# Tokens ahead of the modulation matrix: reordering the opening of an encoder trunk

## The chip, the cores and the metric

The kernel is one program on one core of a Trainium2 chip. The metric is the device time of one execution in microseconds (us). Three runs of the kernel before gave 2377.03, 2378.3 and 2380.01 us; the median, 2378.3 us, is the time before.

In the profile PE is the matmul engine and PEld its weight load, DVE the vector engine, ACT the scalar engine, POOL the GpSimd engine and SP the engine that issues nearly all DMAs.

## The reference

The trunk has two layers (sequence 1024, width 1024, batch 1, all float32). What matters here is the start of the first one:

```
cond = silu(c)                                   # c: 1024 numbers
mod = cond @ w_mod[l] + b_mod[l]                 # w_mod[l]: 1024 x 6144
sh_a, sc_a, gt_a, sh_f, sc_f, gt_f = split(mod)  # six rows of 1024
h = rms_norm(x, g_attn[l]) * (1 + sc_a) + sh_a   # x: 1024 tokens x 1024
proj = h @ w_in[l]                               # w_in[l]: 1024 x 2048
...                                              # three attention groups, w_o, residual
h = rms_norm(x, g_ffn[l]) * (1 + sc_f) + sh_f    # then a SwiGLU FFN, residual
```

Before any projection can begin, a feature needs its shift `sh_a` and scale `sc_a`, that is two columns of `w_mod` multiplied by `cond`, and a token needs its root mean square.

## The kernel before

Everything is held with features on the 128 partitions: `xt[:, n, t]` is token `t` of feature chunk `n` (eight chunks of 128). A float32 product is made of three products of parts: each operand is split into a high part that the PE multiplies and a low part that is the rest, and `mm3` adds high x high, low x high and high x low. `hh` and `hl` are the high and low part of the normalised, modulated `h`; `whi` and `wlo` those of a weight.

The stretch that the change touches is the opening, which is written out by hand: `pin` (L744 to L899) makes PE, ACT, DVE and SP each run their instructions in the order in which the code issues them. POOL has its own order. A wait of one instruction therefore holds everything behind it on the same engine.

In the opening the kernel does the following.

- `load_vecs` issues on POOL's queue four small loads for each layer (bias and gains, 72 rows of 128), and `turn_vecs` transposes them on PE so that a chunk's bias and gain stand on partitions. `turn_vecs(0)` and `turn_vecs(1)` stand together.
- `gm_load(i)` loads a 1 MB tile of `w_mod`: half of the 1024 rows, shift and scale columns of two feature chunks. Eight such tiles, in three buffers, make the 1024 features. `gemv_half(i, kd)` multiplies it by `cond`: for the first `kd` of its four row blocks DVE multiplies and adds into `ga`, and for the rest PE does it with matmuls of one column (`ps_m`). `columns` then adds `ga` with one more set of one-column matmuls, and `gemv_finish` adds the bias and makes the scale `gsc` on DVE. In the trace each of these one-column matmuls of the program stands as two rows.
- `x_load` loads 128 tokens (512 KB). `x_square` sums their squares on ACT, `x_turn_first` transposes them on PE (`ps_x`) and copies them to `xt`, `x_rms` and `spread` make the reciprocal root mean square of the first 512 tokens and spread it over the partitions (`ps_r`, copied to `rb`).
- `h_blocks` makes two chunks of `h`: on DVE `nt` = token x scale x reciprocal root, on ACT `hh` = `nt` + shift, on DVE `hl` = `nt` + shift - `hh`.
- `wc_stage` loads two chunks' rows (512 KB) of the 512 columns of `w_in` for attention group C, `w_high` splits them. `c_first(n)` multiplies chunk `n` of the first 512 tokens with them: three passes of four 128x512 matmuls into the four banks `ps_c`. `a_stage`, `a_high` and `a_first` do the same for two column blocks of group A (`ps_ab`).
- `keep_busy(n)` issues `n` 128x512 matmuls whose result nobody reads (`ps_idle`).

The chunks come in pairs: `gemv_finish(0)`, `h_blocks(0, ..., (0, 1))`, `c_first(0)`, `c_first(1)` and so on. `c_first(4)` is the first product of the fifth chunk; from there on the code of before and after is the same. Later in the opening `gains_load` loads the head gains `g8` (tile `g`) and `c_norm_first` multiplies by them on DVE; `skA` is a 1 MB copy between DRAM buffers that needs a small table `skr`, which POOL stores once a `gm` buffer has come free for it.

Of the kernel before, what the change touches and what calls it, by code (L numbers as in the profile page):

```python
# [10 lines left out]
F32 = mybir.dt.float32  # L11
# [74 lines left out]
def trunk(ctx: ExitStack, tc, A, C, out):  # L86
# [544 lines left out]
    def gemv_half(i, kd=3):  # L631
# [18 lines left out]
        if s:  # L650
            return lambda: columns(gas.pop(p), ones, False, True)

    def gemv_finish(p):
# [33 lines left out]
    def wc_stage(kp):  # L687
        st = stage()
        for dst, v in w_in_src(0, C_COLS, kp)(parts(st, 2)):
            sp.dma_start(dst, v)  # L690
        wcs.append(st)

    def c_first(n, passes=range(3)):

# [58 lines left out]
    wc_stage(0)  # L753
    gm_load(2)
# [20 lines left out]
    keep_busy(10)  # L775
    gemv_half(0)
    gm_load(3)
    wc_stage(1)
    keep_busy(8)
    x_square(0, 0, xns[0][0], rxs[0])  # L780
    x_square(0, 1, xns[0][1], rxs[0])
    columns = gemv_half(1)
    gm_load(4)
    keep_busy(4)
    columns()
    turn_vecs(0, v0)
    turn_vecs(1, v1)
    gemv_finish(0)
    for copy in x_turn_first(xns[0], 0, range(4)):
        copy(dve.tensor_copy)  # L790
    x_square(0, 2, xns[0][2], rxs[0])
    keep_busy(3)
    x_square(0, 3, xns[0][3], rxs[0])
    copies = x_turn_first(xns[0], 1, range(4))
    copies[0](dve.tensor_copy)
    x_rms(rxs[0])
    rows = spread(rxs[0], 0, psl)
    low = w_high()
    copies[1](act.copy)
    keep_busy(6)  # L800
    h_blocks(0, rows, (0, 1), low)
    a_stage(0)
    for copy in copies[2:]:
        copy(act.copy)
# [3 lines left out]
    c_first(0)  # L808
    gemv_half(2, 2)
    gm_load(5)  # L810
    c_first(1, (0, 1))
    low = w_high()
    columns = gemv_half(3, 2)
    gm_load(6)
    columns()
    c_first(1, (2,))
    low()
    wc_stage(2)
    gemv_finish(1)
    a_low = a_high(0)  # L820
    for j in (0, 1):
        xns[1].append(x_load(1, j))
    h_blocks(0, rb, (2, 3))
    c_first(2)
    a_low()
    pssA = [psl.tile([P, 512], F32, name="ps_ab", tag="mm") for _ in range(2)]
    gemv_half(4)
    gm_load(7)
    wc_stage(3)
    for j in (2, 3):  # L830
        xns[1].append(x_load(1, j))
    c_first(3)
    low = w_high()
    columns = gemv_half(5)
    low()
    a_stage(1)
    columns()
    gemv_finish(2)
    a_first(0, 0)
    a_first(0, 1)  # L840
    h_blocks(0, rb, (4, 5))
    c_first(4)
    x_square(1, 0, xns[1][0], rxs[1])
    x_square(1, 1, xns[1][1], rxs[1])
# [1740 lines left out]
```

## Time and profile before

| what | value |
|---|---|
| time, median of three runs | 2378.3 us (2377.03 to 2380.01) |
| the profiled execution's own time | 2376.24 us |
| its span, first to last instruction | 2374.4 us |
| mean granted PE clock | 0.997 |
| PE busy, share of the span | 98% |
| DVE, ACT, POOL busy | 74%, 50%, 33% |
| DMA packets, bytes | 307416, 358.01 MB |

The span is what the profile covers; 1.84 us of the execution's time lie around it. Nearly all operations are issued through one helper, so their source line is L49 and they are told apart by the names of their tiles. A timeline row gives the start, the length of the (merged) group, the engine, the operation, what it writes and reads, its shape, how many instructions it holds, and in brackets how long the engine was idle before it and what ended that.

### The profile page before, as it was taken

To read this page: it belongs to the slowest core of one execution; us is meant where nothing else is said; L and a number is where in the kernel's file an instruction comes from. 1 tells how busy PE (TensorE), PEld (TensorE's weight loads), DVE (VectorE), ACT (ScalarE), POOL (GpSimd) and SP (SyncE) were. 2 spreads that over 40 slices of the span, in tenths; PEclk is the share of its full clock that TensorE was granted. 3 is DMA by queue.
4 is the path that set the end of the run, shared out by engine and by line. 5 is a ranking of instruction groups with operands and counts; after the bars stand their busy time and mean duration, and the time that the engine had idled before them with its cause. 6 is when DMAs were issued, how large, how long until landed. Compare 5 with 4: busy or idle time off the path is not lost. (4 is left out here: it accounts for less than half of the span.)

```text
span 2374.4 us, 33475 instructions
## 1 busy us (share of the span) xinstructions
PE 2327.5 (98%) x11804; PEld 1961.2 (83%) x11804; DVE 1754.3 (74%) x2753; ACT 1184.7 (50%) x2261; POOL 787.0 (33%) x747
## 2 busy tenths in 40 slices
PE   9999999999999999999999999999999999999998
PEld 7888888888788888788888889988888888888886
DVE  6877998868857687595767689987796674537865
ACT  4422888844543333344533158896454333334443
POOL 1530446710344444200145124574025443430001
PEclk9999999999999999999999999999999999999999
DMA  8666407163345444685434861332634443339633
GB/s 279 181 204 207 148 9 206 46 208 104 117 149 164 155 138 151 209 247 178 152 104 132 245 187 28 84 111 80 221 101 130 153 154 107 98 102 292 217 120 111
DMA packets 307416, 358.01 MB, mean 151 GB/s; under 512 B 51996, under 2 KB 223868, under 8 KB 307248
## 3 DMA queue, kind: packets, MB, share of 16 engines
q1 hardware_dynamic: 290752, 346.26, 46.7%
q10 hardware_dynamic: 16128, 9.44, 1.5%
q8 instruction: 93, 1.52, 0.3%
q14 instruction: 75, 0.61, 0.1%
q0 software_dynamic: 368, 0.17, 0.0%
HBM read 270.84 MB, written 88.63 MB: 151 GB/s over the span
## 5 line engine op out<-in xcount | busy, mean ns | idle before, releaser
L49 PE MATMUL ps_d<-wpt 128*128 128x512 f32 x1848 | 423.7, 390 | 1.0 <-ACT wpt L49 0.7
L49 PEld LDWEIGHTS ps_d<-wpt 128*128 128x128 f32 x1848 | 345.7, 188 | 74.4 <-issue 3.0
L49 POOL TENSOR_SCALAR pr<-pr,rs 128x1024 f32<-128x1024 f32 (+2 forms) x248 | 190.4, 783 | 188.3 <-DVE rs L49 170.8
L49 POOL TENSOR_TENSOR sg<-sg,u 128x512 f32<-128x512 f32 x82 | 128.4, 1567 | 349.3 <-ACT sg L49 221.6
L49 PE MATMUL pv<-pt,vs 128*128 128x256 f32 x1088 | 176.0, 296 | 16.5 <-DVE y L49 13.8
L49 DVE TENSOR_TENSOR pt<-T,pt 128x512 fp32r<-128x512 f32 x272 | 177.5, 680 | 7.0 <-ACT pt L49 5.8
L49 ACT CAST wpt<-w 128x512 fp32r<-128x512 f32 x154 | 95.7, 621 | 172.4 <-PE ps_d L49 155.0
L49 ACT CAST pt<-T 128x512 fp32r<-128x512 f32 x272 | 151.6, 586 | 42.5 <-PE T L49 41.0
L49 ACT COPY u<-ps_w 128x512 f32<-128x512 f32 x128 | 75.1, 587 | 193.0 <-PE ps_w L49 190.2
L49 DVE SCALAR_TENSOR_TENSOR acc<-wmt,condT,acc 128x512 f32<-128x512 f32 (+1 forms) x98 | 113.9, 1170 | 75.3 <-DMA wmt<-in_w_mod_dram 74.8
L49 DVE TENSOR_TENSOR wpt<-w,wpt 128x512 fp32r<-128x512 f32 x154 | 108.9, 707 | 81.5 <-ACT wpt L49 81.5
L49 POOL TENSOR_TENSOR wpt<-ws,wpt 128x512 fp32r<-128x512 f32 x80 | 111.1, 1390 | 171.1 <-ACT wpt L49 126.0
L49 PEld LDWEIGHTS pv<-pt,vs 128*128 128x128 f32 x1088 | 142.1, 189 | 29.9 <-DVE y L49 25.5
L49 PE MATMUL T<-identr,pr 128*128 128x128 f32 x1176 | 160.8, 273 | 0.8 <-DVE pt L49 0.4
L49 PEld LDWEIGHTS T<-identr,pr 128*128 128x128 f32 x1176 | 137.8, 140 | 15.5 <-ACT edge L49 1.0
L49 ACT CAST wpt<-ws 128x512 fp32r<-128x512 f32 x176 | 107.7, 622 | 52.7 <-issue 22.9
L49 DVE TENSOR_TENSOR wpt<-graw,wpt 128x512 fp32r<-128x512 f32 x154 | 110.2, 715 | 17.3 <-ACT wpt L49 17.3
L49 ACT CAST wpt<-graw 128x512 fp32r<-128x512 f32 x154 | 95.0, 617 | 54.6 <-DMA graw<-gpd 48.9
L49 DVE TENSOR_TENSOR wpt<-ws,wpt 128x512 fp32r<-128x512 f32 x96 | 84.5, 889 | 47.8 <-ACT wpt L49 47.6
L49 DVE TENSOR_TENSOR ws<-wr 128x512 f32<-128x512 f32 x88 | 81.0, 920 | 50.2 <-POOL wpt L49 46.4
L49 DVE TENSOR_REDUCE rs<-sC 128x1 f32<-128x1024 f32 x88 | 107.2, 1220 | 12.6 <-PE sC L49 11.6
L49 PE MATMUL ps_w<-ht3h,wpt 128*128 128x512 f32 x352 | 108.9, 391 | 2.5 <-ACT sg L49 2.5
(306 smaller groups left out, 5936.5 us busy)
## 6 DMA issues: line engine op xcount, KB each, us to landing
wr<-in_w_gu_dram SPq DMA_DIRECT2D x92, 512.0 KB, 4.3
gpd<-sg SPq DMA_DIRECT2D x154, 256.0 KB, 4.4
graw<-gpd SPq DMA_DIRECT2D x76, 512.0 KB, 3.6
w<-in_w_down_dram SPq DMA_DIRECT2D x110, 256.0 KB, 5.3
wmt<-in_w_mod_dram SPq DMA_DIRECT2D x48, 512.0 KB, 5.6
qk<-qkd SPq DMA_DIRECT2D x44, 512.0 KB, 7.0
wst<-in_w_o_dram SPq DMA_DIRECT2D x32, 512.0 KB, 4.2
wmt<-in_w_mod_dram SPq DMA_DIRECT2D x64, 256.0 KB, 4.1
```

The lines of the kernel that those rows point to most:

```text
L49: ins = op(*args, **kwargs)
```

## The change

The change rewrites the opening up to `c_first(4)`.

- The first 512 tokens are loaded ahead of `w_mod`. The first four feature chunks get their own `w_mod` tiles (`gm_one(n)`: all 1024 rows, shift and scale columns of one chunk, 1 MB in four loads of 256 KB, rows of 512 bytes), and their rows of `w_in` come one chunk at a time (`wc_half`). The other four chunks keep the tiles of before.
- The class `One` does a chunk's gemv: `add` on DVE, `col` and `total` on PE. In chunk 0 six of the eight row blocks go to PE, in chunks 1 to 3 three.
- `turn` multiplies tokens by the reciprocal root ahead of the scale. `finish` then makes `hh` in one ACT instruction (scale and shift together); POOL makes the same value in full (`ht`) and `low` subtracts.
- The fillers become 8, 2, 1, 1, 2, 3, 3 and 2 in place of 10, 8, 4, 3 and 6. One `a_first` moves between other work, and `gemv_half(4)` puts two row blocks on PE in place of one.

```diff
+    def gm_one(n):
+        gm = gms["one", n] = stp.tile([P, KC, 2, P], F32, name="gm", tag="gm", bufs=3)
+        for k in (0, 4):
+            for g in range(2):
+                c0 = g * 1024 + n * P
+                rows = A["w_mod"][0, k * P : (k + 4) * P, c0 : c0 + P]
+                sp.dma_start(
+                    gm[:, k : k + 4, g, :], rows.rearrange("(k p) n -> p k n", p=P)
+                )
+    class One:
...
+        def turn(self, rows):
+            self.xr = stp2.tile([P, H], F32, name="nt", tag="nt", bufs=3)
+            dve.tensor_tensor(out=self.xr, in0=xt[:, self.n, 0:H], in1=rows, op=ALU.mult)
+        def finish(self):
...
+            dve.tensor_tensor(
+                out=m[:, :, n : n + 1], in0=self.ps[:, :, None], in1=v[:, :, n : n + 1],
+                op=ALU.add,
+            )
+            dve.scalar_tensor_tensor(
+                out=sc, in0=mods[0][:, 8 + n : 9 + n], scalar=1.0,
+                in1=vecs[0][:, 48 + n : 49 + n], op0=ALU.add, op1=ALU.mult,
+            )
+            act.activation(hh[:, n, 0:H], self.xr, AF.Identity, bias=sh, scale=sc)
+            self.t = stp2.tile([P, H], F32, name="ht", tag="ht", bufs=1)
+            pool.tensor_scalar(
+                out=self.t, in0=self.xr, scalar1=sc, scalar2=sh, op0=ALU.mult, op1=ALU.add
+            )
+        def low(self):
+            sub(hl[:, self.n, 0:H], self.t, f32(hh[:, self.n, 0:H]))
...
-    gm_load(0)
-    gm_load(1)
     xns = [[x_load(0, j) for j in range(4)], []]
+    gm_one(0)
+    wc_half(0)
+    gm_one(1)
+    wc_half(1)
+    gm_one(2)
+    wc_half(2)
     v0, v1 = load_vecs(0), load_vecs(1)
...
+    for n in range(1, 4):
+        two.add(0, 1, 2)
+        low = w_high_half(n)
+        c_first(n - 1, (0,))
+        two.col(3)
+        c_first(n - 1, (2,))
+        two.add(4, 5)
+        two.col(6)
+        c_first(n - 1, (1,))
+        two.col(7)
+        two.total()
+        two.finish()
+        if n < 3:
+            keep_busy(3)
+            one, two = two, One(n + 1)
+            two.turn(rb)
+            low()
+            one.low()
+            if n == 1:
+                a_stage(0)
+            gm_load(3 + n)
+        else:
+            low()
+            two.low()
...
+    keep_busy(2)
     c_first(4)
```

Where the instructions stand now. PE's program before, from the transposed vectors to the first products of group C (`pst` a transposed vector tile, `ps_x` transposed tokens, `ps_r` the spread root, `ps_c` group C, `ps_m` a gemv):

```order
L49 MATMUL pst<-identr,v_138 128x72
L49 MATMUL pst<-identr,v_143 128x72
L49 MATMUL ps_x<-identr,xn 128x128 x16
L49 MATMUL ps_idle<-identr 128x512 x3
L49 MATMUL ps_x<-identr,xn 128x128 x16
L49 MATMUL ps_r<-identr,rx 128x128 x4
L49 MATMUL ps_idle<-identr 128x512 x6
L49 MATMUL ps_c<-whi,hh 128x512 x4
```

PE's program after, the same place:

```order
L49 MATMUL ps_x<-identr,xn 128x128 x16
L49 MATMUL pst<-identr,v_152 128x72
L49 MATMUL pst<-identr,v_157 128x72
L49 MATMUL ps_idle<-identr 128x512 x2
L49 MATMUL ps_x<-identr,xn 128x128 x8
L49 MATMUL ps_m<-condT,gm 128x1 x4
L49 MATMUL ps_x<-identr,xn 128x128 x4
L49 MATMUL ps_r<-identr,rx 128x128 x4
L49 MATMUL ps_m<-condT,gm 128x1 x4
L49 MATMUL ps_x<-identr,xn 128x128 x4
L49 MATMUL ps_idle<-identr 128x512
L49 MATMUL ps_m<-condT,gm 128x1 x4
```

The first half of the token transposes moved ahead of the vectors, the second half and the spread stand behind them, and the first chunk's gemv is spread between them.

PE's program after, from the end of the first chunk's gemv through one turn of the loop over chunks:

```order
L49 MATMUL ps_m<-onesr,ga 128x1 x2
L49 MATMUL ps_idle<-identr 128x512 x2
L49 MATMUL ps_c<-whi,hh 128x512 x4
L49 MATMUL ps_m<-condT,gm 128x1 x2
L49 MATMUL ps_c<-wlo,hh 128x512 x4
L49 MATMUL ps_m<-condT,gm 128x1 x2
L49 MATMUL ps_c<-whi,hl 128x512 x4
L49 MATMUL ps_m<-condT,gm 128x1 x2
L49 MATMUL ps_m<-onesr,ga 128x1 x2
L49 MATMUL ps_idle<-identr 128x512 x3
```

Each turn holds one chunk's three passes and the next chunk's gemv, and ends with three fillers ahead of the next chunk's first product; before, two chunks' passes followed one another.

The difference on PE at the fifth chunk (`ps_ab` is group A, the last `ps_c` rows are `c_first(4)`):

```order
 L49 MATMUL ps_ab<-hh,hl 128x512
 L49 MATMUL ps_ab<-hl,hh 128x512
+L49 MATMUL ps_m<-onesr,ga 128x1 x4
+L49 MATMUL ps_idle<-identr 128x512 x2
 L49 MATMUL ps_c<-whi,hh 128x512 x4
 L49 MATMUL ps_c<-whi,hl 128x512 x4
```

The last matmuls of the third pair's gemv, which stood ahead of both `a_first`, now stand behind them, right ahead of `c_first(4)`, with two fillers between.

SP's queue before, from the last weight loads of the opening but one to the copy `skA`:

```order
L49 DMA wst<-in_w_in_dram 128x8x128 x2
L49 DMA g_518<-in_gq_ax_dram 128x6x64
L49 DMA g_518<-in_gk_ax_dram 128x2x64
L49 DMA cst<-const_rope_dram 128x128 x4
L49 DMA t_530<-in_t_table_dram 32x6
L49 DMA skA_91<-skr 512x1x512
```

SP's queue after, the same place:

```order
L49 DMA wst<-in_w_in_dram 128x8x128
L49 DMA skA_91<-skr 512x1x512
L49 DMA wst<-in_w_in_dram 128x8x128
L49 DMA g_555<-in_gq_ax_dram 128x6x64
L49 DMA g_555<-in_gk_ax_dram 128x2x64
L49 DMA cst<-const_rope_dram 128x128 x4
```

The copy `skA`, which waits for POOL's table, moved from behind the head gains to ahead of them.

More of the change, by code (lines that the diff above doesn't have):

```diff
@@ L774, in trunk @@
     dve.tensor_copy(condT, pst[:, :KC])
[L775 to L778, printed above, removed]
     keep_busy(8)
[L780 to L785, printed above, removed]
+    for j in range(4):
+        x_square(0, j, xns[0][j], rxs[0])
+    for copy in x_turn_first(xns[0], 0, range(4)):
+        copy(dve.tensor_copy)
     turn_vecs(0, v0)
     turn_vecs(1, v1)
[L788 to L790 removed]
@@ L791, in trunk @@
[L791 to L794, printed above, removed]
+    keep_busy(2)
+    one = One(0)
+    copies = x_turn_first(xns[0], 1, (0, 1))
     copies[0](dve.tensor_copy)
     x_rms(rxs[0])
+    copies[1](act.copy)
+    one.col(0, 1)
+    x_turn_first(xns[0], 1, (2,))[0](act.copy)
     rows = spread(rxs[0], 0, psl)
[L798 to L801, printed above, removed]
@@ L802, in trunk @@
-    a_stage(0)
-    for copy in copies[2:]:
-        copy(act.copy)
+    one.turn(rows)
+    one.col(2, 3)
+    x_turn_first(xns[0], 1, (3,))[0](act.copy)
     rb = stp2.tile([P, H], F32, name="rb", tag="rb", bufs=2)
     act.copy(rb, rows)
-    pssC = [psl.tile([P, 512], F32, name="ps_c", tag="mm") for _ in range(T0)]
[L808 to L811, printed above, removed]
-    low = w_high()
[L813 to L821, printed above, removed]
-        xns[1].append(x_load(1, j))
[L823 to L833, printed above, removed]
+    one.add(4, 5)
+    keep_busy(1)
+    one.col(6, 7)
+    keep_busy(1)
+    one.total()
@@ L834, in trunk @@
+    wcs = wcs[2:]
+    wc_stage(2)
+    a_high(0)()
+    gm_load(6)
+    wc_stage(3)
+    pssA = [psl.tile([P, 512], F32, name="ps_ab", tag="mm") for _ in range(2)]
+    gemv_half(4, 2)
+    c_first(3, (0, 1))
+    low = w_high()
+    gm_load(7)
+    for j in range(4):
+        xns[1].append(x_load(1, j))
+    c_first(3, (2,))
+    a_first(0, 0)
     columns = gemv_half(5)
```

63 lines of the change are left out of this document (59 added, 4 removed).

## The prediction

> **What bounds the kernel.** I read the page's busy shares first, then the busy times by stretch, then PE's timeline of the opening with what ended its waits, then the other engines at those places.
>
> ```profile
> span 2374.4 us, 33475 instructions
> PE 2327.5 (98%) x11804; PEld 1961.2 (83%) x11804; DVE 1754.3 (74%) x2753; ACT 1184.7 (50%) x2261; POOL 787.0 (33%) x747
> ```
>
> The profiled execution took 2376.24 us, 2.1 us under the median 2378.3. PE is full. The next view gives the busy time of each engine in a stretch (PE first); the last three fields are the granted clock, the DMA share and GB/s.
>
> ```profile
> 5.00:10.00 5.00, 5.00 (x23) 4.13 (x22) 1.99 (x3) 0.00 (x0) 1.54 (x4) 1.00 1.07 355
> 27.00:28.00 1.00, 1.00 (x6) 0.83 (x5) 1.00 (x2) 0.00 (x0) 0.00 (x0) 1.00 1.14 291
> 45.00:50.00 5.00, 5.00 (x28) 4.27 (x27) 4.82 (x7) 4.35 (x8) 1.75 (x2) 1.00 0.79 274
> 70.00:75.00 5.00, 5.00 (x24) 4.10 (x23) 3.72 (x7) 1.84 (x5) 0.72 (x1) 1.00 0.61 209
> ```
>
> From the fifth chunk on (44.97 us, below) PE has no gap up to 75 us, and the code behind that point is the same in both kernels. So I take it that what the change is worth is read at one place: when `c_first(4)` starts. PE's timeline up to there:
>
> ```profile
> 12.81 1.05 PE L49 MATMUL ps_m<-onesr,ga 128*128 128x1 f32 x8 [0.63 <-DVE ga L49]
> 13.72 0.32 PE L49 MATMUL pst<-identr,v 72*128 72x72 f32 x2
> 13.88 3.23 PE L49 MATMUL ps_x<-identr,xn 128*128 128x128 f32 x16
> 16.76 1.37 PE L49 MATMUL ps_idle<-identr 128*128 128x512 f32 x3
> 17.97 1.91 PE L49 MATMUL ps_x<-identr,xn 128*128 128x128 f32 x16
> 19.72 0.60 PE L49 MATMUL ps_r<-identr,rx 128*128 128x128 f32 x4
> ...
> 21.92 1.18 PE L49 MATMUL ps_c<-whi,hh 128*128 128x512 f32 x4 [0.20 <-ACT hh L49]
> 22.93 1.07 PE L49 MATMUL ps_c<-whi,hl 128*128 128x512 f32 x4
> 23.84 1.19 PE L49 MATMUL ps_c<-wlo,hh 128*128 128x512 f32 x4
> 24.87 1.84 PE L49 MATMUL ps_m<-condT,gm 128*128 128x1 f32 x16
> 26.57 1.16 PE L49 MATMUL ps_c<-whi,hh 128*128 128x512 f32 x4
> ...
> 30.19 1.03 PE L49 MATMUL ps_m<-onesr,ga 128*128 128x1 f32 x8
> 31.08 1.83 PE L49 MATMUL ps_c<-wlo,hh 128*128 128x512 f32 x4
> 33.21 1.89 PE L49 MATMUL ps_c<-whi,hh 128*128 128x512 f32 x4 [0.30 <-ACT hh L49]
> 34.94 1.09 PE L49 MATMUL ps_c<-whi,hl 128*128 128x512 f32 x4
> ...
> 42.12 0.48 PE L49 MATMUL ps_ab<-hh 128*128 128x512 f32 x1
> ...
> 44.97 1.07 PE L49 MATMUL ps_c<-whi,hh 128*128 128x512 f32 x4
> ```
>
> PE has 31 fillers (10 + 8 + 4 + 3 + 6 in the code) ahead of 21.92 and from there to 44.97 (23.05 us) only useful work with 0.30 us of waiting. Prices by the distance from one start to the next: four 128x512 products 0.91 (22.93 to 23.84), so 0.23 each; a one-column matmul of the program (two trace rows) 0.21 (24.87 to 26.57 for eight); a token transpose 0.11 (17.97 to 19.72 for 16), 0.18 in the slower stretch at 13.88; the spread 0.35; a filler there 0.46 (1.37 for three).
>
> The slower stretches are seen in the granted clock. The next view counts the one-column matmuls alone (first value after the length: their PE time; third from the end: the clock):
>
> ```profile
> 10.87:14.28 3.41, 1.33 (x11) 1.16 (x10) 0.00 (x0) 1.00 1.03 376
> 14.28:17.70 3.42, 0.00 (x0) 0.00 (x0) 0.15 (x1) 0.50 1.05 370
> 24.52:27.94 3.42, 1.84 (x16) 1.94 (x16) 0.00 (x0) 1.00 1.11 327
> 27.94:31.35 3.41, 2.73 (x24) 2.83 (x24) 0.10 (x1) 1.00 1.05 321
> 31.35:34.76 3.41, 0.00 (x0) 0.00 (x0) 0.07 (x1) 0.50 1.02 325
> ```
>
> The clock halves for 3.41 us after a stretch in which one-column matmuls and waits together held 1.33 + 0.63 = 1.96 us, or 2.73 us. It does not after 1.84 us.
>
> **The change, part by part.** I follow the new PE order to `c_first(4)`.
>
> *Loads.* From the first use of 1 MB of matrix and of the first tokens I get when data can be there:
>
> ```profile
> 6.61 0.49 DVE L49 TENSOR_SCALAR ga<-gm,condT 128x512 f32<-128x512 f32 x1 [3.12 <-DMA gm<-in_w_mod_dram]
> 24.88 2.33 DVE L49 SCALAR_TENSOR_TENSOR ga<-gm,condT,ga 128x512 f32<-128x512 f32 x3
> ```
>
> 1.05 MB at 355 GB/s are 2.95 us, so data run 3.65 us behind the clock. Tokens (2.1 MB) are there at 9.6; the first chunk's tile at 12.5 to 13.1 (355, or 291 GB/s, the lowest rate shown, for it), and each further 1.31 MB takes 3.7 to 4.4 us: chunk 3 by 23.6 to 26. All of that is ahead of its use below, so the loads themselves cost nothing; the earlier tokens and tiles are the change's gain only if nothing else is late.
>
> *What is late instead: the small vectors.* In the new order eight token transposes, the spread and the whole first gemv stand behind both `turn_vecs`, layer 1's too. POOL issues those loads one by one:
>
> ```profile
> 5.52 0.50 POOL L49 DMA_DIRECT2D v<-in_g_group_dram  x1
> DMA to landing us min/median/max: 3.8/5.9/6.6
> ```
>
> (the second line is the tile view of `v`). The last one lands at 5.52 + 5.9 to 6.6, 11.4 to 12.1; I take 11.8. Before, PE came to them at 13.72 and waited for nothing. Now PE is through the first 16 transposes near 9 and stands. From 11.8: vectors 0.2, two fillers and eight transposes at half clock (the wait halves it) 0.9 + 1.4, gives 14.3; four one-column matmuls 0.85, four transposes 0.44, spread 0.35, then 0.85, 0.44, filler 0.23, 0.85, filler 0.23, total of two 0.43, gives 19.0.
>
> *The way from a gemv's end to the first product.* Its stations are seen once before:
>
> ```profile
> 31.25 0.16 DVE L49 TENSOR_TENSOR mod<-ps_m,vecs 128x4 f32<-128x4 f32 x1 [2.91 <-PE ps_m L49]
> 31.45 0.16 DVE L49 SCALAR_TENSOR_TENSOR gsc<-mod,vecs 128x2 f32<-128x2 f32 x1
> 31.65 1.42 DVE L49 SCALAR_TENSOR_TENSOR nt<-xt,gsc,rb 128x512 f32<-128x512 f32 x2
> 32.44 1.39 ACT L49 ACTIVATE hh<-nt,mod 128x512 fp32r<-128x512 f32 x2 [1.20 <-DVE nt L49]
> ```
>
> From the gemv's end (31.08) 0.17 to DVE, 0.40 to `nt`, 0.71 for one `nt`, 0.08 to ACT, 0.77 to PE (33.21): 2.1 us. The high part in one pass drops the 0.71, leaving 1.4. So `c_first(0)` starts at 20.4 at full clock; all transposes and the spread between 14.3 and 19.0 at half clock would add 1.2; I take 20.8. That is 1.1 earlier than 21.92.
>
> *The loop.* One turn is 12 products 2.73, eight one-column matmuls 1.70 and the 1.4 of the way, in which three fillers (0.7) stand but no useful work: 5.8 us. Before, this way stood behind other products and cost 0.20 and 0.30. Two turns end at 32.5. The third has `gemv_half(4)` behind it (1.70), which covers the way: 2.73 + 1.70 + 1.70, 38.6. DVE does not bind: per turn three 128x512 operations of 0.71 (`nt` row) and five half-wide additions, which lie between half and all of 0.78 (row at 24.88), and 0.4, that is 4.5 to 6.4; I take the lower end, since the work is halved, and it lies within 5.8.
>
> *To the fifth chunk.* `c_first(3)` 2.73, `a_first` 1.43 twice (12 products from 42.12 to 44.97), `gemv_half(5)` 0.85 and its total 0.85: 45.3 + 0.6 from rounding and changes of operand (the same list of before adds up 0.8 short of its 23.05), 45.9. Then the full way of 2.1, since the chunks 4 and 5 still use `h_blocks`: 48.0. Before, both `a_first` covered it; now two fillers do. Against 44.97 that is +3.0.
>
> *Clock.* Stretches with over 1.9 us of one-column matmuls and waiting: the end of the run-up (0.85 + 0.43 + 1.4 less fillers), and the third turn's end with `gemv_half(4)` (2.5). The first one halves the clock in the loop, of which 59% are products, price 0.59 x 3.41 / 2 = 1.0; the second hits `c_first(3)`, price as at 31.35 before, where 31.08 and 33.21 took 1.83 and 1.73 for 0.91 each: 1.7. Before's own such stretch is in its 23.05. Sum +5.7; it can be 0 stretches (+3.0 less 0.4) or four (about +8.5).
>
> *POOL's* new `ht` (four times) lies beside the loop, where POOL had nothing; `hl` needs it two passes later. If it were late it would cost PE under 1 us a turn. The low part's two halves of `w_high` replace equal work.
>
> Sum: 2376.24 + 5.7 = 2381.9 for the profiled kind of execution, 2378.3 + 5.7 = **2384.0** as a median.
>
> **Rivals.**
>
> *The clock stays full.* Then the run-up is 1.0 shorter (fillers 0.5, transposes 0.9), its 0.4 for half clock falls, and no stretch is charged: 48.0 - 1.4 = 46.6, +1.6, 2379.9. For it: the worst stretches inside the loop stand at 1.2 of one-column work and 0.7 of uncovered wait, about the 1.84 that passed. Against it: 2.73 and 1.96 did not pass. The Trainium skill's page "TensorE: Matmul & The Clock Gate", section "Why this matters for your kernels", says that the clock holds as long as no idle gap of more than about 3 us opens between bursts of matmuls; by it this rival would be the case, as the only such gap is the wait for the vectors. The trace disagrees: half clock began at 14.28 behind a gap of 0.63 and at 31.35 behind none. Chance 0.17.
>
> *The small vectors land with the tokens, by 9.0* (not slower). The four tokens' loads are fewer and longer packets than matrix rows, and POOL's loads may slip through faster. Then there is no wait and no half clock in the run-up: the tokens of 9.6 are transposed by 10.6, the same 4.7 and 1.4 follow, `c_first(0)` is at 16.7, and one stretch falls: 50.7 - 4.1 - 1.0 = 45.6, +0.6, 2378.9. It decides from a landing before 10.9, where the loss falls under what can be told. Against it: 5.9 us in the median from issue to landing, and POOL issues the last at 5.52 in either kernel. Chance 0.14.
>
> *The head gains come too late.* `skA` moved ahead of them on SP and waits for POOL's table, which waits for the third pair's gemv.
>
> ```profile
> 41.66 0.52 POOL L49 DMA_DIRECT2D gm<-in_rpb_na_dram  x1 [35.12 <-PE ps_m L49]
> ...
> 52.28 0.57 SPq L49 DMA_DIRECT2D g<-in_gq_ax_dram  x1
> 66.08 1.20 POOL L49 TENSOR_SCALAR g<-g 128x384 f32<-128x384 f32 x1 [15.93 <-DMA g<-in_gq_ax_dram]
> 73.50 0.69 DVE L49 TENSOR_TENSOR gm<-gm,g 128x512 f32<-128x512 f32 x1
> ```
>
> With that gemv 5.5 later the gains are issued near 58.7, and the 1 MB copy ahead of them takes 0 to 3.6 us (291 GB/s): scaled by 73.7 to 77.3, wanted at 79.2. I take no wait. If the copy runs at half that rate, DVE stands and PE behind it: +3 more, 2387. Chance 0.11.
>
> *The loads are not ahead at all* (the change does not do what it says): The DMA share stands at 1.07 in the row for 5 to 10 us, and the tile now comes in four pieces. If its last piece lands later than 17.5, where the last row blocks are wanted, all is delayed by as much; at +3, 2387. Against it: tokens and tile are the first 3.1 MB in the queue. Chance 0.08.
>
> **How the numbers follow.** The forecast has 0.50, with 2381.5 to 2386.5 as its own range. Runs of this kernel lie within 3 us, so about 0.2% (4.76 us) can be told from no change: the bound is 2383.06. Of the forecast's half some 0.33 lie above it; with the last two rivals (0.19) and 0.02 of the first, slower has 0.54. Of the vector rival I leave 0.06 for faster. The rest, 0.40, is no change. The range goes from 2378.5, just under the vector rival, to 2389, four half-clock stretches or both late rivals.
>
> **What would show it.** In the changed profile: PE idle up to some 11.8 ahead of `pst<-identr,v`; the first `ps_c` near 20.8; idle near 0.7 us ahead of `ps_c<-whi,hh` in chunks 1 and 2, ended by ACT `hh`; `c_first(4)` near 50.7, with over 1 us of idle ended by ACT `hh`; DMA share falling under 0.7 somewhere from 34 to 40 us, as SP waits for buffers that the later gemvs free; two half-clock stretches behind the run-up. It is wrong if `c_first(0)` starts before 18, if the chunks follow at under 5 us, or if PE shows new waits behind 75 us.

## The result and the profile after

The changed kernel is slightly slower. Thirteen executions of each kernel gave a median of 2387.22 us (2381.27 to 2396.3) against 2378.41 (2375.61 to 2384.23); the ratio after to before is 1.0039, with a 95% interval of 1.003 to 1.0047. The executions of after spread over 15 us, those of before over 9. The spread goes with the mean granted PE clock of an execution. The five executions of after with a clock of 0.997 or 0.998 took 2381.27 to 2384.23 us, the eight with 0.990 to 0.995 took 2384.88 to 2396.3. For the kernel before, 67 executions that ran beside the experiments gave a median of 2376.6 at 0.997 or more (44 of them) and 2379.7 below (23).

The profiled execution of after took 2389.74 us, with a mean granted clock of 0.993. Its page:

```profile
span 2388.0 us, 33542 instructions
PE 2337.7 (98%) x11815; PEld 1968.8 (82%) x11815; DVE 1753.7 (73%) x2765; ACT 1184.9 (50%) x2263; POOL 782.9 (33%) x751
```

PE is busy 10.2 us longer than before, with 11 rows more, and the span is 13.6 longer. So most of the loss stands in the records as longer work and not as waiting. PE's timeline of the opening (start, length, operation, tiles, shape, count, and the idle time before with its releaser):

```profile
11.47 0.25 PE L49 MATMUL pst<-identr,v 72*128 72x72 f32 x1 [2.02 <-DMA v<-in_g_group_dram]
...
17.30 1.71 PE L49 MATMUL ps_m<-condT,gm 128*128 128x1 f32 x8
18.87 1.09 PE L49 MATMUL ps_x<-identr,xn 128*128 128x128 f32 x4
...
24.46 2.08 PE L49 MATMUL ps_c<-whi,hh 128*128 128x512 f32 x4 [0.23 <-ACT hh L49]
...
32.50 1.20 PE L49 MATMUL ps_c<-whi,hh 128*128 128x512 f32 x4 [0.49 <-ACT hh L49]
...
38.53 1.20 PE L49 MATMUL ps_c<-whi,hh 128*128 128x512 f32 x4 [0.49 <-ACT hh L49]
...
53.00 0.95 PE L49 MATMUL ps_m<-onesr,ga 128*128 128x1 f32 x8
53.81 0.71 PE L49 MATMUL ps_idle<-identr 128*128 128x512 f32 x2
55.94 1.90 PE L49 MATMUL ps_c<-whi,hh 128*128 128x512 f32 x4 [1.42 <-ACT hh L49]
```

The first product is 2.54 us later than before (24.46 against 21.92) and the fifth chunk's 10.97 later (55.94 against 44.97). The next view cuts the same time along the clock's steps of 3.41 us and counts the one-column matmuls alone (second number: their PE time; third from the end: the granted clock):

```profile
8.39:11.80 3.41, 0.00 (x0) 0.00 (x0) 0.00 (x0) 1.00 1.19 289
11.80:15.21 3.41, 1.21 (x7) 1.42 (x7) 0.00 (x0) 0.50 1.14 309
15.21:18.63 3.42, 1.82 (x10) 1.94 (x10) 0.00 (x0) 0.50 1.14 309
18.63:22.04 3.41, 2.08 (x10) 2.38 (x11) 0.00 (x0) 0.50 0.98 260
22.04:25.45 3.41, 0.85 (x4) 0.94 (x4) 0.16 (x1) 0.50 0.65 188
25.45:28.87 3.42, 0.85 (x4) 1.42 (x5) 0.00 (x0) 0.50 0.69 201
28.87:32.28 3.41, 1.45 (x12) 1.46 (x11) 0.16 (x1) 1.00 0.00 0
42.52:45.93 3.41, 2.53 (x23) 2.44 (x22) 0.16 (x1) 1.00 0.23 24
45.93:49.35 3.42, 0.00 (x0) 0.00 (x0) 0.00 (x0) 0.50 0.95 245
```

Behind the stretch with the wait for the vectors the clock is at half for five stretches in a row, 17.1 us, up to 28.87. It halves once more behind the 2.53 us of one-column matmuls at the third turn's end, and once at the fifth chunk (56.17 to 59.59). Before had two single stretches in the opening. At half clock the one-column matmuls are slower too: the eight rows at 17.30 take 1.57 us to the next start, where eight rows at full clock (53.00 to 53.81) take 0.81.

From the 10.97 us at the start of `c_first(4)` to the 13.6 of the span two more parts are added. `c_first(4)` itself stands in the last of these half-clock stretches and takes 1.7 us longer. At the head gains PE then loses 0.9 us more (SP's, POOL's and DVE's timeline):

```profile
63.48 0.73 SPq L49 DMA_DIRECT2D skA<-skr  x1
64.31 3.36 SPq L49 DMA_DIRECT2D wst<-in_w_in_dram  x1
67.72 5.25 SPq L49 DMA_DIRECT2D g<-in_gq_ax_dram  x1
85.82 1.20 POOL L49 TENSOR_SCALAR g<-g 128x384 f32<-128x384 f32 x1 [26.41 <-DMA g<-in_gq_ax_dram]
87.05 0.69 DVE L49 TENSOR_TENSOR gm<-gm,g 128x512 f32<-128x512 f32 x1 [0.96 <-POOL g L49]
```

The gains are issued behind the copy `skA` and a weight, POOL gets them 18.1 us after their issue (13.8 in before), and DVE stands 0.96 us for them.

### The profile page after: what moved, and what is told of

It reads as the page before. It is cut to its first block, busy times and chain, and to the rows that moved or that the text cites. A ratio compares the mean times of both kernels' runs of the same rounds, so it can differ in the third digit from the quotient of the medians.

```text
span 2388.0 us, 33542 instructions
## 1 busy us (share of the span) xinstructions
PE 2337.7 (98%) x11815; PEld 1968.8 (82%) x11815; DVE 1753.7 (73%) x2765; ACT 1184.9 (50%) x2263; POOL 782.9 (33%) x751
## 5 line engine op out<-in xcount | busy, mean ns | idle before, releaser
L49 POOL TENSOR_TENSOR sg<-sg,u 128x512 f32<-128x512 f32 x82 | 118.7, 1448 | 350.5 <-ACT sg L49 221.6
L49 PE MATMUL ps_w<-h22h,wpt 128*128 128x512 f32 x352 | 108.9, 391 | 2.4 <-ACT u L49 1.4
```

The source lines that it names most:

```text
L49: ins = op(*args, **kwargs)
```

## The experiments

Four theories stood against each other. A: the wait for the vectors takes the clock down, and that costs more than the wait. B: the uncovered way from a gemv's end to the next first product is the loss. C: the loads set the pace. D, formed after the first four runs: the head gains' landing is a floor. The medians, with the ratio to the kernel before that ran beside them:

| kernel | median us (lowest to highest, executions) | ratio, 95% interval |
|---|---|---|
| after | 2387.22 (2381.27 to 2396.3, 13) | 1.0039 (1.003 to 1.0047) |
| e1: layer 1's vectors later | 2380.11 (2377.95 to 2392.45, 12) | 1.002 (1.0007 to 1.0032) |
| e2: nine fillers in the wait | 2388.78 (2380.67 to 2391.4, 7) | 1.0038 (1.0024 to 1.0051) |
| e3: cover at the fifth chunk | 2385.08 (2382.74 to 2393.47, 6) | 1.0039 (1.0025 to 1.0054) |
| e4: high part in two passes | 2388.99 (2386.51 to 2393.68, 5) | 1.0049 (1.0036 to 1.0062) |
| e5: gains ahead of a weight | 2390.79 (2388.26 to 2394.02, 5) | 1.0053 (1.0041 to 1.0065) |
| e6: e1 and e5 | 2389.73 (2383.31 to 2394.5, 6) | 1.0047 (1.0032 to 1.0062) |
| e7: e6 and e3 | 2390.41 (2385.89 to 2392.95, 5) | 1.0048 (1.0036 to 1.006) |
| e8: e7 and a covered loop | 2386.7 (2385.83 to 2394.92, 6) | 1.0041 (1.0029 to 1.0054) |
| e9: gains behind that weight | 2385.9 (2378.78 to 2393.58, 6) | 1.0041 (1.0027 to 1.0055) |
| e10: e1 and e9 | 2377.3 (2373.43 to 2386.82, 12) | 1.0005 (0.9995 to 1.0015) |
| e11: e10, cover, covered loop, first gemv | 2375.4 (2372.88 to 2387.81, 12) | 0.9996 (0.9986 to 1.0007) |
| e12: e11 with the loop's work gathered | 2379.5 (2373.84 to 2383.03, 11) | 1.0002 (0.9993 to 1.0011) |

### e1 and e2: the wait and the clock

e1 moves the one transpose that PE waited for; e2 leaves it and fills the wait.

```diff
 # e1
     turn_vecs(0, v0)
-    turn_vecs(1, v1)
     keep_busy(2)
...
     wcs = wcs[2:]
+    turn_vecs(1, v1)
     wc_stage(2)
 # e2
     turn_vecs(0, v0)
+    keep_busy(9)
     turn_vecs(1, v1)
```

> Edit of the changed kernel: the transpose of layer 1's small vectors, the one that PE waited 2.02 us for at 11.47 us, moves behind the loop over chunks; layer 0's stays. Theory A (half clock: the wait takes the clock down, and at half clock products, transposes and one-column matmuls all cost double, so the wait costs more than its own length): the clock stays full in the run-up, c_first(0) goes from 24.46 to between 19.5 and 21, the time falls by 3.5 to 5 us. Theory B (the uncovered way from a gemv's end to the next chunk's first product is the loss; the run-up matters little): c_first(0) comes about 2 us earlier, by the wait alone, and the time falls by 1.5 to 2.5. Theory C (the loads set it): PE stands instead ahead of the first one-column matmul, whose tile landed at 11.63 and 12.50, the clock falls all the same, c_first(0) starts after 22.5 and the time falls by less than 1.5.

> Edit of the changed kernel: nine more fillers (0.23 us each at full clock) stand ahead of the transpose of layer 1's vectors, so that PE waits with work; nothing else moves and nothing is ready earlier. Theory A (half clock): the clock is full from 11.8 on, c_first(0) goes from 24.46 to 19.1 to 21, the time falls by 3.5 to 5 us although no data come earlier. Theory B (uncovered way): c_first(0) moves by less than 1 us and the time by less than 1. Theory C (the half clock comes from the one-column matmuls of the first gemv, with or without the wait): the clock halves one stretch later, c_first(0) comes 1 to 2 us earlier.

PE's timeline of e1, and DVE's row for the head gains:

```profile
9.04 0.26 PE L49 MATMUL pst<-identr,v 72*128 72x72 f32 x1 [0.20 <-DMA v<-in_g_group_dram]
...
11.29 0.83 PE L49 MATMUL ps_m<-condT,gm 128*128 128x1 f32 x6 [0.23 <-DMA gm<-in_w_mod_dram]
...
18.94 2.08 PE L49 MATMUL ps_c<-whi,hh 128*128 128x512 f32 x4 [0.23 <-ACT hh L49]
...
49.33 1.20 PE L49 MATMUL ps_c<-whi,hh 128*128 128x512 f32 x4 [1.42 <-ACT hh L49]
...
81.71 0.69 DVE L49 TENSOR_TENSOR gm<-gm,g 128x512 f32<-128x512 f32 x1 [3.77 <-DMA g<-in_gk_ax_dram]
```

And the same rows of e2:

```profile
11.51 0.25 PE L49 MATMUL pst<-identr,v 72*128 72x72 f32 x1 [0.48 <-DMA v<-in_g_group_dram]
...
19.14 1.19 PE L49 MATMUL ps_c<-whi,hh 128*128 128x512 f32 x4 [0.72 <-ACT hh L49]
...
48.58 1.19 PE L49 MATMUL ps_c<-whi,hh 128*128 128x512 f32 x4 [1.42 <-ACT hh L49]
...
80.41 0.69 DVE L49 TENSOR_TENSOR gm<-gm,g 128x512 f32<-128x512 f32 x1 [3.24 <-POOL g L49]
```

In e1 the wait is gone, `c_first(0)` starts 5.5 us earlier than in after's profile, and the median falls by 7.1 us (by 0.19 points of the ratio, 4.5 us), of which 2.0 us belong to another place (see e10). Theory C falls: PE waits 0.23 us for the first tile. Two half-clock stretches in a row still follow, at 14.1 and 17.5. In e2's profiled execution the clock stays full up to 37.7, and `c_first(0)` stands at 19.14 although no data came earlier. So the clock accounts for most of the 5 us there, as A said, and B's bound of 1 us fell in this execution. The median of e2 did not fall, against A's 3.5 to 5: four of its seven executions took 2388.78 to 2391.4, at clocks of 0.993 to 0.996. So filling the wait alone did not help in four of seven. No profile shows these four, so where they lose is open; two of them have 0.996, more than their time fits.

Both profiles show what the profile of after had hidden. From `c_first(4)` to the gains' product on DVE, which stood at 73.50 before, e1 loses 3.9 us more (from 4.36 to 8.21) and e2 3.3 more (from 3.61 to 6.91).

### e3 and e4: the uncovered way

```diff
 # e3
-    a_first(0, 0)
     columns = gemv_half(5)
     low()
     a_stage(1)
-    a_first(0, 1)
     columns()
     gemv_finish(2)
+    a_first(0, 0)
+    a_first(0, 1)
     h_blocks(0, rb, (4, 5))
-    keep_busy(2)
     c_first(4)
 # e4, class One: turn keeps rows; finish and low become
+            dve.scalar_tensor_tensor(
+                out=self.t, in0=xt[:, n, 0:H], scalar=sc, in1=self.rows,
+                op0=ALU.mult, op1=ALU.mult,
+            )
+            act.activation(hh[:, n, 0:H], self.t, AF.Identity, bias=sh)
...
+            dve.scalar_tensor_tensor(
+                out=hl[:, self.n, 0:H], in0=self.t, scalar=self.sh,
+                in1=f32(hh[:, self.n, 0:H]), op0=ALU.add, op1=ALU.subtract,
+            )
```

> Edit of the changed kernel at the fifth chunk: the order of before comes back, the third pair's gemv is totalled ahead of both a_first, and the two fillers ahead of c_first(4) go. Theory B (uncovered way): the wait of 1.42 us ahead of c_first(4) and the 0.47 us of fillers go, the time falls by 1.7 to 2.2, and by up to 3.7 if the half-clock stretch in which c_first(4) stood (1.7) goes with them. Theory A (half clock): the wait goes, but another stretch takes the half clock, and the time falls by less than 1.

> Edit of the changed kernel that undoes one part: in chunks 0 to 3 the tokens are again multiplied by scale and reciprocal root on DVE behind the gemv, ACT adds the shift, DVE makes the low part from both, POOL takes no part. Theory B (uncovered way): the way of chunks 0 to 2 gets 0.6 to 0.7 us longer each and nothing covers it, c_first(4) comes 1.9 us later, the time rises by 1.5 to 2.5, more by 1.7 for each further half-clock stretch. Theory A: the longer waits fall into stretches that are at half clock anyway and the time rises by less than 1. If the high part in one pass was worth nothing, as it would be where other products cover the way, there is no difference.

PE's timeline of e3:

```profile
11.52 0.25 PE L49 MATMUL pst<-identr,v 72*128 72x72 f32 x1 [2.17 <-DMA v<-in_g_group_dram]
...
19.15 2.08 PE L49 MATMUL ps_c<-whi,hh 128*128 128x512 f32 x4 [0.34 <-ACT hh L49]
...
47.74 1.07 PE L49 MATMUL ps_c<-whi,hh 128*128 128x512 f32 x4
...
58.88 0.62 PE L49 MATMUL ps_r<-identr,rx 128*128 128x128 f32 x4 [0.75 <-DVE mod L49]
...
60.61 1.19 PE L49 MATMUL ps_c<-whi,hh 128*128 128x512 f32 x4 [0.68 <-ACT hh L49]
```

The wait of 1.42 us and the fillers are gone, and DVE, with no slack left, takes 1.43 back at 59 to 61 us. Later DVE stands 3.0 us for the gains, as in e1 and e2. The ratio is that of after, so the time shows no gain. The first two rows say something else: the code up to there is that of after, the wait is even longer, and yet the clock stayed full behind it, up to 17.85, and the first product came at 19.15 in place of 24.46 (one half-clock stretch follows, from 17.85 to 21.26). Whether the wait halves the clock differs from one execution to the next.

PE's timeline of e4:

```profile
20.17 1.52 PE L49 MATMUL ps_c<-whi,hh 128*128 128x512 f32 x4 [1.49 <-ACT hh L49]
...
38.93 1.19 PE L49 MATMUL ps_c<-whi,hh 128*128 128x512 f32 x4 [1.18 <-ACT hh L49]
```

At full clock the way is 0.77 us longer (1.49 against e2's 0.72) and 0.69 longer (1.18 against 0.49), as B said. At half clock it is no less: the wait was 0.50 there, and from the first filler to the product 2.12 us passed (28.17 to 30.29), where e10 below, with one pass, took 1.43 at half clock (26.62 to 28.05) without a wait. So in the profiles the high part in one pass is worth 0.7 us per uncovered chunk at either clock, against what A said. The median rose by 1.8 us, with intervals that overlap, although e4 too is spared the 2.0 us described under e10.

### e5 to e8: the head gains in the wrong place

```diff
 # e5 (e6: with e1's edit; e7: with e3's as well)
     low()
+    g8 = gains_load(ccp, 0)
     a_stage(1)
...
     wab = [w_ab(0, 0)]
-    g8 = gains_load(ccp, 0)
 # e8, on e7: ahead of the loop
-    two.turn(rb)
-    low()
-    one.low()
...
+    two.col(4, 5)
     keep_busy(2)
 # e8: in the loop
-        two.add(0, 1, 2)
+        two.add(0, 1)
+        low()
+        one.low()
+        two.add(2, 3)
+        two.turn(rb)
         low = w_high_half(n)
         c_first(n - 1, (0,))
-        two.col(3)
+        two.col(6)
         c_first(n - 1, (2,))
-        two.add(4, 5)
-        two.col(6)
-        c_first(n - 1, (1,))
         two.col(7)
         two.total()
         two.finish()
+        c_first(n - 1, (1,))
         if n < 3:
-            keep_busy(3)
             one, two = two, One(n + 1)
-            two.turn(rb)
-            low()
-            one.low()
+            two.col(4, 5)
```

> Edit of the changed kernel: only the load of the head gains (with the rope tables behind it) moves ahead of the fifth weight load on SP, so ahead of the copy skA. Theory D (the gains' landing is a floor under which an earlier PE does not come: in the runs with nine more fillers and with the later vector transpose DVE stood 3.2 and 3.7 us for the scaled gains, in the changed kernel 0.96): DVE no longer waits for POOL's g, PE is no later at 100 us than at 70 us against before, and executions without half clock fall from about +6.9 to +3.8 against before; those with many half-clock stretches fall by 1 or less. The median falls by 1 to 3 us against the changed kernel. Rival: the copy, now behind the gains, makes a weight load late instead and the time stays within 0.7.

> Edit of the changed kernel: layer 1's vectors transposed behind the loop, and the head gains loaded ahead of the copy. Theory D: the shift against before stays at what it is at c_first(4), 4.4 us or less, where with the later transpose alone it rose from 4.5 to 8.2 between 75 and 90 us; the median falls by 3 to 4 us against that run's 2380.1, to 2376 to 2378, level with before. If the gains are no floor but the wait at 80 us only showed slack, no change: 2379 to 2381.

> The edit before this one, and the order of before at the fifth chunk (the third pair's gemv totalled ahead of both a_first, no fillers). Theory B (uncovered way): the wait of 1.42 and the fillers' 0.47 go, 1.9 us less. But in the run with this order alone PE then stood 0.75 us for DVE's mod and 0.68 for ACT's hh at 59 to 61 us, so that DVE is the next bound and 1.4 of it come back: by that the median is only 0.5 us less, and by theory B alone 1.9 less.

> The edit before this one, and in the loop over chunks the way from a gemv's end to the next chunk's first product is covered: a gemv is totalled ahead of the last pass of the chunk before, four of its row blocks go to DVE and four to PE, two of these ahead of the next first product in place of the three fillers. Theory B: a turn falls from 6.03 us to 4.9 to 5.3, no wait of over 0.2 us ahead of c_first(1) and c_first(2), c_first(4) comes 1.5 to 2.2 us earlier, and the median is 1.5 to 2 less. Rival: DVE, with the same operations in shorter turns, becomes the bound, the turn stays over 5.6, and nothing is left of it at 100 us.

All four medians are 2386.7 us or more. Two of e7's waits show why (engine, tile, what it waited for: us in total, times, longest); e5, e6 and e8 have the same pair:

```profile
PE ps_c L49 <- ACT hh L49: 11.0, 4, 9.3
...
ACT hh L49 <- DMA wst<-in_w_in_dram: 8.6, 1, 8.6
```

The gains went ahead of the fifth weight load, that weight came late, ACT waited for it, and everything behind ACT waited with it. The rival named for e5, a weight that comes late, came true, though by the gains themselves, and at 7.2 to 9.3 us of PE's time. The floor itself was gone: none of the four has a wait of DVE for the gains. e7 stood at 45.13 for `c_first(4)`, 0.16 us behind before, ahead of this wait. In e8 the loop's turns took 5.00 us (`c_first(1)` at 29.43, `c_first(2)` at 34.43), against 6.03 in after, without a wait ahead of them.

### e9 and e10: the gains behind that weight

```diff
 # e9 (e10: with e1's edit)
     low()
     a_stage(1)
+    g8 = gains_load(ccp, 0)
...
     wab = [w_ab(0, 0)]
-    g8 = gains_load(ccp, 0)
```

> Edit of the changed kernel: the load of the head gains and rope tables moves ahead of the copy skA, but behind the fifth weight load (in the runs with the gains ahead of that weight, PE stood 7.6 to 9.3 us for ACT's hh, ACT for the weight). Theory D (gains are a floor): DVE does not wait for POOL's g, no PE wait of over 1 us stands for that weight, the shift against before at 100 us is what it is at 70; executions with few half-clock stretches (granted clock 0.997 or 0.998) come from 2381 to 2383 down to 2378 to 2380, the median falls by 1 to 3 against the changed kernel. Rival: the next weight, behind the gains, or the copy is late in its place, and PE gets a new wait of 2 us or more behind 75 us.

> The edit before this one, and layer 1's vectors transposed behind the loop. Theory D: the shift of 4.4 at c_first(4) is no longer raised by 3.7 between 75 and 90 us; the median comes to 2376 to 2378.5, against 2380.1 with the later transpose alone. If the floor has another cause than the gains, it stays at 2379 to 2381.

PE's, POOL's and DVE's timeline of e9:

```profile
49.89 1.20 PE L49 MATMUL ps_c<-whi,hh 128*128 128x512 f32 x4 [1.42 <-ACT hh L49]
...
66.60 1.50 POOL L49 TENSOR_SCALAR g<-g 128x384 f32<-128x384 f32 x1 [13.54 <-DMA g<-in_gq_ax_dram]
...
78.56 0.69 DVE L49 TENSOR_TENSOR gm<-gm,g 128x512 f32<-128x512 f32 x1
```

DVE no longer waits, and against before the delay is 4.92 us at `c_first(4)` and 5.06 at the gains (78.56 against 73.50): theory D holds in its mechanism. How much of it shows in the time depends on the clock. With the vectors' wait in place (e9 against after) the ratio stays, 1.0041 and 1.0039. Five of e9's six executions have a clock of 0.995 or less, and an execution that the half clock delays wants the gains later too: DVE's wait for them was 0.96 us in after and 3.24 in e2. With the transpose moved (e10 against e1) the median falls by 2.8 us and the ratio by 0.15 points, 3.6 us. From e9 to e10, the vectors' transpose alone, the median falls by 8.6. e10 is level with before. Its own profiled execution is its longest (2386.82 us): PE still waits 1.43 us there, for layer 0's vectors, and eight half-clock stretches follow in a row, from 17.1 to 44.4.

A part of these gains stands far behind the opening. PE's timeline of after, and of e1 at the same matmul:

```profile
219.59 0.47 PE L49 MATMUL ps_ab<-hh,whi 128*128 128x512 f32 x1 [1.73 <-DVE own L49]
...
212.31 0.39 PE L49 MATMUL ps_ab<-hh,whi 128*128 128x512 f32 x1
```

In the profiles of before, after, e2, e3, e5 and e9 PE waits 1.73 us here for a DVE operation. In those of e4 and of all kernels with e1's edit it does not, and PE's delay against before falls by 2.0 us at this matmul (in e1 from 8.16 to 6.18). So of the 8.6 us about 6.6 are left for the opening. Without this place, by estimate from the medians, e10 would stand about 3 us above before, and e11 (the next section) about 1. Why the wait goes is not shown: the order of PE's instructions here is the same in all of them.

### e11 and e12: a version that is level, and how long the half clock lasts

```diff
 # e11, on e8 with e9's place for the gains: the first gemv
-    one.col(0, 1)
     x_turn_first(xns[0], 1, (2,))[0](act.copy)
+    x_turn_first(xns[0], 1, (3,))[0](act.copy)
     rows = spread(rxs[0], 0, psl)
+    one.add(0, 1)
     one.turn(rows)
-    one.col(2, 3)
-    x_turn_first(xns[0], 1, (3,))[0](act.copy)
     rb = stp2.tile([P, H], F32, name="rb", tag="rb", bufs=2)
     act.copy(rb, rows)
-    one.add(4, 5)
-    keep_busy(1)
+    one.add(2, 3)
+    keep_busy(2)
+    one.col(4, 5)
+    keep_busy(2)
     one.col(6, 7)
-    keep_busy(1)
+    keep_busy(2)
     one.total()
 # e12, on e11: the loop
-        c_first(n - 1, (0,))
-        two.col(6)
-        c_first(n - 1, (2,))
-        two.col(7)
+        c_first(n - 1, (0, 2))
+        if n == 1:
+            two.col(6, 7)
         two.total()
...
-            two.col(4, 5)
+            two.col(4, 5, 6, 7)
```

> The edit before this one, the order of before at the fifth chunk, the loop with covered ways (its turns took 5.00 us in the run before, with the gains still in the wrong place), and in the first chunk four row blocks on DVE in place of two, with fillers between the four on PE, so that one-column matmuls and waits hold less of a stretch. Theory A and B together: c_first(0) between 16.5 and 18.5, turns of 5.0, c_first(4) 1 to 3 us ahead of before's 44.97 in executions without half clock in the run-up, no floor at 80 us; median 2374 to 2377, so level with before or 1 to 3 us faster. Rival: half clock comes back in the run-up all the same, c_first(4) at 46 or later, median 2378 or more.

> The edit before this one, with the work of a turn in another order: two passes of products stand together, then the total, the third pass, and the next gemv's four row blocks together, in place of one-column matmuls behind every pass. Theory A2 (the half clock holds on: in the traces so far it came back to full only behind a stretch of 3.41 us with 2.58 us or more of products, transposes and fillers, and stayed half at 2.35 or less; the changed kernel's loop and that of the run before hold one-column matmuls in every stretch at half clock, 1.56 us of them in the run before, so that its eleven half-clock stretches in a row ended only at the fifth chunk): now two passes are 3.64 us at half clock and fill a stretch, so no row of half-clock stretches ahead of 55 us is longer than four, no execution is above 2382 us where the run before had one of 2387.8, turns at full clock stay at 5.0, and the median is 2373 to 2375.5. Rival (the length of the row depends on what set it off, or on chance): rows of more than four come back, and executions over 2385. Third case: the four row blocks together, 1.7 us, are enough to halve the clock in each turn, and the median rises to 2378 or more.

e11 has the lowest median of all, 2375.4 us against 2376.5 for before, but its interval spans 1: it beats the changed kernel and is level with before, with the 2.0 us of the later place in its favour. Eleven of twelve executions took 2372.88 to 2376.76. The twelfth, 2387.81, is the profiled one, and one-column matmuls by stretch show why (columns as above):

```profile
14.27:17.68 3.41, 1.95 (x15) 2.06 (x16) 0.16 (x1) 1.00 1.14 305
17.68:21.10 3.42, 1.21 (x6) 1.19 (x7) 0.00 (x0) 0.51 1.19 301
31.33:34.75 3.42, 1.71 (x10) 1.95 (x10) 0.00 (x0) 0.50 0.93 305
```

The clock fell at 17.7 and came back at 55.3, eleven stretches later, while PE was busy all the time; `c_first(4)` stood at 59.65, as the rival had said (46 or later), though not the median. I counted, in the fourteen profiles, the time of each 3.41 us stretch that PE spent in wide work (products, transposes, fillers), leaving out one-column matmuls and waits, each instruction counted up to the next one's start. The fall with which every profile ends is left out. In all 33 other falls to half clock the stretch ahead held 1.72 us of wide work or less. In all 33 returns it held 2.58 or more, and 43 stretches at half clock with up to 2.77 stayed there, so that from 2.58 to 2.77 both were seen (e12's expectation put the limit for staying at 2.35, which was too low). At full clock nothing fell from above 1.72, and some stretches down to 1.41 did not fall. Between 1.73 and 2.57 the clock stayed as it was: 232 stretches at full clock did not fall, and 25 at half clock did not come back. So the fall and the return have different limits. e11's loop holds 1.56 us of one-column work and 1.85 of wide work in five of its eleven half-clock stretches, between the limits, and all but one of the others stay under 2.58 as well. The same loop in e8 also began at half clock, but one of its stretches held 2.71, the clock came back at 26.4, and the next three stretches, with 1.80 to 2.24, kept it full. So this loop can run at either clock, and which it is depends on how the stretches cut it.

e12 gathers the work to make stretches of wide work alone:

```profile
16.39:19.80 3.41, 2.02 (x8) 1.85 (x8) 0.10 (x1) 0.50 1.14 309
19.80:23.21 3.41, 0.00 (x0) 0.33 (x1) 0.00 (x0) 0.50 1.14 312
23.21:26.63 3.42, 2.55 (x23) 2.64 (x23) 0.16 (x1) 1.00 0.92 243
26.63:30.04 3.41, 1.21 (x7) 1.13 (x6) 0.00 (x0) 0.50 0.50 135
30.04:33.45 3.41, 0.85 (x4) 1.14 (x5) 0.16 (x1) 0.50 1.10 363
33.45:36.86 3.41, 1.84 (x16) 1.92 (x16) 0.00 (x0) 1.00 0.86 273
```

The rows of half clock are at most two long, as A2 said. But the gathered one-column work, 2.55 us at 23.21, sets off a new one, the third case. The longest execution is 2383.03, where e11 had 2387.81 (A2 had said 2382 at most), and the median is 2379.5. But the executions of before that ran beside e12 had 2378.2 where those beside e11 had 2376.5, and the two ratios, 1.0002 and 0.9996, have intervals that overlap, so the times don't show that gathering costs anything. In these two profiles it trades one long row for two short ones.

## Why the prediction was right or wrong

- **The sum.** Slower was right, and 2387.2 lies in the range that goes to 2389, 3.2 us above the 2384.0 and a little above the 2386.5 at which the forecast's own range ends. That it came so near is partly luck. Five executions of after lie at 2381.3 to 2384.2 and eight at 2384.9 to 2396.3, and the profiled one lost 13.6 us of span where the sum has 5.7: it denied the floor at the gains, and it priced the clock too low for that execution.
- **The one place to read.** That "what the change is worth is read at one place: when `c_first(4)` starts" was wrong. e1 and e2 lose 3.3 to 3.9 us more behind it, at the head gains, and near 205 us some of the kernels win 2.0 (see e10). After's `c_first(4)` started at 55.94 and not near 50.7. Of these 5.2 us, 3.7 stand ahead of `c_first(0)` and 1.2 in the first turn beyond the half clock that the sum had for it.
- **The vectors.** The wait up to 11.8 came at 11.47, 2.02 us long. That it is the part of the change that costs most is shown by e10 against e9, 8.6 us, or 6.6 without the place near 205 us. How much of it is the clock and how much the wait itself is shown by single profiles only (e2 and e3 against after); e2's median did not confirm it.
- **The clock.** This term was mis-sized. The limit for the fall was near: 1.96 us of one-column work and waits together, where falls began at 1.69 (3.41 less 1.72). The step that failed is the price: each fall was charged for one stretch of 3.41 us, and the one-column matmuls at 0.21 as at full clock. The profile of after has seven half-clock stretches in place of two, five of them in a row, and eight one-column rows take 1.57 us there in place of 0.81. Hence `c_first(0)` at 24.46 and not 20.8, while e3, with the clock full up to 17.85, had 19.15.
- **The loop.** 5.8 us per turn was 6.03 at full clock (32.50 to 38.53), with waits of 0.49; the first turn, at half clock up to 28.87, took 8.04.
- **The fifth chunk.** The full way of 2.1 us was 2.13 (53.81 to 55.94), 1.42 of it waiting. From `c_first(3)` to `c_first(4)` the sum has 9.4 (48.0 less 38.6); 11.03 were measured, 1.67 of them for the half clock in `c_first(3)`. The parts that the prediction names add up to 45.9 and not to 45.3, so its 48.0 has nothing in it for rounding after all, and nothing was needed. That the way costs what it showed did not follow: e3 took it away and DVE took 1.43 back.
- **One pass for the high part.** The 0.71 saved per chunk is confirmed, 0.69 and 0.77 in e4.
- **The gains.** "I take no wait" failed. The copy ahead of them was priced at 0 to 3.6 us on a landing at 73.7 to 77.3. They were issued at 67.72, not 58.7, because the copy waited for POOL's table until 63.48 and a weight's issue held SP for 3.36, and POOL had them 18.1 us later. The copy's bytes are not shown as the cause of the late landing: e9, with no copy ahead of the gains, had 18.4, and why 13.8 became 18 stays open. In after everything else was late too, so DVE stood 0.96; in e2 3.24. This rival was given 0.11; its wait came, and e9 and e10 show that it hangs on where the gains stand in the queue.
- **The loads.** Right: no PE wait for tokens or tiles in after. (The 291 GB/s were not "the lowest rate shown": two rows of the same view have 274 and 209, at DMA shares of 0.79 and 0.61. The loads came in time all the same.) The DMA share did fall, but to 0.01 in 30 to 34 us and 0.47 in 40 to 45, not in 34 to 40:

```profile
30.00:34.00 4.00, 3.51 (x22) 2.78 (x21) 2.12 (x5) 1.32 (x2) 1.59 (x1) 1.00 0.01 3
34.00:40.00 6.00, 5.51 (x33) 4.50 (x32) 4.40 (x11) 1.32 (x2) 1.59 (x1) 1.00 1.00 313
40.00:45.00 5.00, 5.00 (x38) 4.65 (x38) 3.31 (x10) 1.31 (x2) 1.08 (x1) 1.00 0.47 149
```

- **The rival "the clock stays full"** gave 2379.9 us. The five executions at 0.997 and more took 2381.3 to 2384.2, which would fit that rival's +1.6 with the gains' 3 us on top; no profile of after at this clock shows it.

What stays open: which stretches halve the clock in the executions that were not profiled, e2's four long ones above all, and why two of those, at a clock of 0.996, took 6 and 8 us longer than the longest of e2's other three; also why a wait near 205 us is there in some kernels and not in others.

## What to carry to other kernels

Price a wait on PE by what it does to the granted clock, and ask not only what takes the clock down but what brings it back: a loop that mixes one-column matmuls evenly with products can stay at half clock for as long as it lasts. When a stage ahead is made faster or slower, follow every DMA whose issue moved in its queue up to its first use, even tens of microseconds on: a floor there hides as long as something else is late. Small loads that are wanted by later code only should not stand in the path of the first products.

## What the runs showed of the hardware that was not expected

- The fall to half clock and the return have different limits: 1.72 us of wide work or less in 3.41 us ahead of each of 33 falls, 2.58 or more ahead of each of 33 returns, in the fourteen profiles. Between them the clock stayed as it was, and half clock lasted up to eleven stretches (37.6 us).
- The same code with the same wait of 2.0 to 2.2 us halved the clock in one execution (after) and not in another (e3; nor in e4, where it was 2.85). The steps of 3.41 us begin at 8.39 us in the one and at 7.61 in the other, so that the wait fell into one step, which was left with 1.40 us of wide work, or was split over two, with 1.65 and 2.10. The Trainium skill's page "TensorE: Matmul & The Clock Gate", section "Part 1: The HAM clock gate (the "warmup" mystery)", says that the window is free-running and its phase differs from run to run; these two traces agree.
- The gains with the rope tables are little data in small rows, and slow: from their issue to POOL's start 13.8 us passed in before (52.28 to 66.08), 18.4 in e9 (48.22 to 66.60), 18.1 in after. Put ahead of a 512 KB weight, they made ACT wait 7.1 to 8.6 us for it.
